# adaLN vectors in small turns between the projections, and w_o's first weights loaded before the attention

## The chip, the cores and the metric

The kernel runs on one NeuronCore of a Trainium2 chip. The metric is the device time of one execution in microseconds. Three runs of the kernel before took 2390.59, 2391.88 and 2393.76 us, median 2391.88.

## The reference, cut to what matters

Two layers over 1024 latent tokens of width 1024. Each layer modulates its input with vectors made from the condition, mixes tokens, adds and normalises, and does the same once more with a SwiGLU feed-forward. Layer 0 mixes by differential attention over 256 context tokens and the 1024 latent ones, layer 1 by pooling.

```
def adaln_params(cond, w_mod, b_mod):
    m = silu(cond) @ w_mod + b_mod                 # 1024 -> 6 * 1024
    return split(m, 6)                             # shift, scale, gate, twice
for i in (0, 1):
    sh1, sc1, g1, sh2, sc2, g2 = adaln_params(c, w_mod[i], b_mod[i])
    hx = x * (1 + sc1) + sh1
    if i == 0:
        csh1, csc1, ... = adaln_params(c_ctx, w_mod[0], b_mod[0])
        hc = ctx * (1 + csc1) + csh1
        k, v = project of hc (256 tokens) and hx (1024 tokens);  q = project of hx
        q, k (latent part) = rope(q), rope(k)
        per head: o = softmax(q1 k1) v - lam * softmax(q2 k2) v   # 8 heads, 2 maps of 64 features
        y = (rms_norm(o) * subln_g * 0.2) @ w_o
    else:
        y = pooling(hx)
    x = layer_norm(ALPHA * x + g1 * y)
    x = layer_norm(ALPHA * x + g2 * swiglu(x * (1 + sc2) + sh2))
```

## The kernel before, in words

Features lie on the partitions and tokens along the free axis. Every fp32 operand of a large product is split into a high part (a cast to fp32r) and a low part (the rest), and a product is three matmuls, high by high, high by low and low by high. A weight tile of 1024 x 128 gives 8 x 3 = 24 matmuls for a span of 512 tokens; this is called a product here.

The stages follow one another: a start in which the latent tokens are modulated and the first keys and queries are made beside it; the projections, a list `steps` of (kind, group, spans) with kind 0 for q, 1 for k and 2 for v; the attention over 8 heads; w_o; the feed-forward, then layer 1. Before the change `steps` takes the rest of q group 0, then groups 1 and 2 of q, half of v, the context and latent spans of k, q group 3 and the other half of v. The weights of a step come through `split_w` (L130): a load of 512 KB from SP into `wr` (two buffers), the high part `wh` on ACT, the low part `wl` on DVE. `finish_qk` (L178) does the rotary on DVE (`ta`, `tb`) and GpSimd, splits the result into `ot` and stores it from ACT's queue. Products go into 8 PSUM banks with the tag `mm`, which `pg` below shares.

Twelve of layer 0's adaLN vectors' pieces of 512 columns, the first four for c_ctx and eight for c, are made between the projections. `between()` (L284) is called after each span and at two of the ten token tiles of v. It takes one piece from the list `rest` and calls `gemv_half` (L102): four loads of 512 KB of `gw`, two buffers; eight operations on DVE (L112 the first, L114 the others) that add w_mod's rows times the condition into `gacc`; four matmuls `pg` (L117) with a matrix of ones that add gacc over the partitions; and an addition on DVE (L118). With the fifth call `context()` modulates the context tokens.

In the attention pools `pq` and `pb` hold kk, qd, vv and the work tiles. When it ends these are released, and pools `pz` (with zT, 4 MB), `phx` and `pf` take memory. `raw` (4 buffers of 512 KB, for w_o's and the feed-forward's weights and for layer 1's gw) and `aop` (3 buffers, the split weights made by `form`) are in `pf`, so `w_o` (L609) first loads and forms weights when the attention's memory is free. w_o goes by d, 128 output features at a time; layer 1's pieces `gemv1(0)` and `gemv1(1)` stand behind d = 1 and d = 4.

The source is not the order of the program. A scheduler puts each engine's instructions in an order of its own, in which each engine works strictly one after the other, and pools decide which tile lies on which memory; an instruction waits for whoever last used its buffer. Loads are issued by SP, the projections' stores by ACT.

Of the kernel before, what the change touches and what calls it, by code (L numbers as in the profile page):

```python
# [43 lines left out]
def backbone(ctx: ExitStack, tc: tile.TileContext, a: dict, out: bass.AP):  # L44
# [56 lines left out]

    def gemv_half(pool, psum, pstag, l, b, tags, bufs, j=0):  # L102

        acc = pool.tile([P, 512], F32, name="gacc", tag=tags[0], bufs=bufs[0])
        for k2 in range(KT // 2):
            wt = pool.tile([P, 2, 512], F32, name="gw", tag=tags[1], bufs=bufs[1])
            SP.dma_start(wt, a["w_mod"][l, k2 * 2 * P:(k2 + 1) * 2 * P, b * 512:(b + 1) * 512]
                         .rearrange("(k p) f -> p k f", p=P))
            for i in range(2):
                k = 2 * k2 + i  # L110
                if k == 0:
                    V.tensor_scalar(acc, wt[:, i, :], sc_sb[:, 0, j:j + 1], None, ALU.mult)  # L112
                else:
                    V.scalar_tensor_tensor(acc, wt[:, i, :], sc_sb[:, k, j:j + 1], acc, ALU.mult, ALU.add)  # L114
        pg = psum.tile([P, 4, P], F32, name="pg", tag=pstag)
        for i in range(4):
            PE.matmul(pg[:, i, :], lhsT=acc[:, i * P:(i + 1) * P], rhs=ones_f, start=True, stop=True)  # L117
        V.tensor_tensor((modx if j else modv[l])[:, b * 4:(b + 1) * 4], pg[:, :, 0], bmod[:, l, b * 4:(b + 1) * 4], ALU.add)  # L118

# [3 lines left out]
    with ExitStack() as actx:  # L123
# [28 lines left out]
        def project_v(g, parts):  # L152
            for tt in list(range(2, NTT)) + [0, 1]:
                if tt in (4, 7):
                    between()
                ts_ = slice(tt * P, (tt + 1) * P)
                ps = psA.tile([P, 512], F32, name="mm", tag="mm")
                for k in range(KT):
                    wh, wl = parts[k]
                    PE.matmul(ps, lhsT=hT_hi[:, k, ts_], rhs=wh, start=(k == 0), stop=False)  # L160
                    PE.matmul(ps, lhsT=hT_hi[:, k, ts_], rhs=wl, start=False, stop=False)  # L161
                    PE.matmul(ps, lhsT=hT_lo[:, k, ts_], rhs=wh, start=False, stop=(k == KT - 1))  # L162
                vt = pa.tile([P, 4, P], F32, name="vt", tag="vt", bufs=3)
                S.copy(vt, ps.rearrange("p (h e) -> p h e", e=P))
                S.dma_start(v_d[g][:, :, tt].rearrange("h p e -> p h e"), vt)
# [37 lines left out]
        def project_qk(kind, g, spans, w):  # L203
            for (t0, n) in spans:
                pp = []
                for s in range(2):
                    ps = psA.tile([P, 512], F32, name="mm", tag="mm")
                    for k in range(KT):
                        mm3(ps, w[s], k, t0, n)
                    pp.append(ps)  # L210
                finish_qk(kind, g, t0, n, pp)
                between()

# [67 lines left out]

        rest = [(b, 1) for b in range(4)] + [None] + [(b, 0) for b in range(4, 12)]

        def between():  # L284
            if rest:
                v = rest.pop(0)
                if len(rest) == 10:
                    load_context()
                if v is None:
                    context()  # L290
                else:
                    gemv_half(pa, psA, "mm", 0, v[0], ("gacc", "gw"), (2, 2), v[1])
# [32 lines left out]
    with ExitStack() as bctx:  # L325
# [90 lines left out]
        for h in range(NH):  # L416
# [54 lines left out]
    def parts(hi, lo, src, eng=None):
        S.copy(hi, src)  # L472
        (eng or V).tensor_tensor(lo, src, hi.bitcast(F32), ALU.subtract)  # L473

    def form(src):

        t = pf.tile([P, 2, 4, P], F32R, name="aop", tag="aop", bufs=AOP)
        parts(t[:, 0], t[:, 1], src)
        return t

# [349 lines left out]
    def pool_group(t0, n, g):  # L830
# [156 lines left out]
```

## Time and profile before

| | |
|---|---|
| median of 3 runs | 2391.88 us |
| profiled execution | 2393.9 us, of which the span from first to last instruction is 2392.1 |
| TensorE matmul busy | 2262.7 us, 95% of the span |
| VectorE busy | 1704.9 us, 71% |
| ScalarE, GpSimd busy | 932.9 us, 39%; 624.5 us, 26% |
| mean DMA rate over the span | 99 GB/s |
| chain of waits, by engine | PE 77%, DVE 13%, DMA 5% |

L12 is line 12 of the kernel. PE is TensorE, DVE is VectorE, ACT is ScalarE, POOL is GpSimd and SP is SyncE, which issues loads. The chain is the work that ended last, followed back from the end; its shares say how much of the span each engine or line had on that path. A timeline row gives the start, the time of a run of like instructions, and in brackets how long the engine was idle before it and whose end released it. PEclk is the granted clock of TensorE as a share of 2.4 GHz.

### The profile page before, as it was taken

What the parts mean: (1) busy time and instruction counts of PE and PEld (TensorE: products, weight loads), DVE (VectorE), ACT (ScalarE), POOL (GpSimd) and SP (SyncE); (2) the same over time, 40 slices, a digit from 0 to 9 for tenths busy, and PEclk for the clock granted to TensorE, in tenths of its full rate; (3) what the DMA queues carried; (4) which work ended last, traced back from release to release, by engine and by line L of the source; (5) the groups of instructions that cost most, each with busy time, mean ns of one, the idle gap of its engine ahead of it and who ended that gap; (6) DMA issues with size and microseconds to landing.
All of it is one profiled execution on the core that took longest, in us unless ns stands there. A gap on an engine that the chain in (4) does not pass through costs nothing.

```text
span 2392.1 us, 31056 instructions
## 1 busy us (share of the span) xinstructions
PE 2262.7 (95%) x11800; PEld 1924.2 (80%) x11800; DVE 1704.9 (71%) x2580; ACT 932.9 (39%) x1635; POOL 624.5 (26%) x618
## 2 busy tenths in 40 slices
PE   5879899999999997999999999999799999999997
PEld 4668787999999786888888888898588888888886
DVE  7664622899998589777777777767966666666678
ACT  3213112787877265222222222437522222222242
POOL 3432322444444043111111111202511111111122
PEclk9989999999999999999999999999899999999999
DMA  7767636523321431322222222213011111111121
GB/s 265 239 210 221 208 87 180 171 69 109 89 78 36 150 114 58 112 88 88 86 84 86 83 85 88 88 33 90 21 62 53 53 51 51 51 52 54 53 89 71
DMA packets 100918, 236.64 MB, mean 99 GB/s; under 512 B 9376, under 2 KB 27424, under 8 KB 99616
## 3 DMA queue, kind: packets, MB, share of 16 engines
q1 hardware_dynamic: 78688, 210.53, 27.7%
q10 hardware_dynamic: 22080, 24.12, 3.5%
q8 instruction: 93, 1.52, 0.3%
q14 instruction: 57, 0.47, 0.1%
HBM read 206.30 MB, written 28.31 MB: 98 GB/s over the span
## 4 chain that ended last, share of the span: by engine, by line
PE 77%; DVE 13%; DMA 5%; ACT 2%; issue 2%; POOL 1%; DVEq 0%; ACTq 0%; SPq 0%; POOLq 0%
PE mm L598 18%; PE mm L597 18%; PE mm L596 18%; PE s L345 6%; PE misc L376 6%; DMA gw<-in_w_mod 3%; PE misc L369 3%; DVE gacc L114 2%; PE mm L161 1%; PE mm L162 1%; PE mm L160 1%; DVE zT L601 1%; DVE aop L473 1%; DVE acc L236 1%; PE mm L170 1%
## 5 line engine op out<-in xcount | busy, mean ns | idle before, releaser
L596 PE MATMUL mm<-H,aop 128*128 128x512 f32 x1232 | 483.6, 393 | 18.0 <-ACT aop L472 10.5
L598 PE MATMUL mm<-H,aop 128*128 128x512 f32 x1232 | 481.8, 392 | 7.1 <-DVE aop L473 7.1
L597 PE MATMUL mm<-H,aop 128*128 128x512 f32 x1232 | 482.6, 392 | 3.3 <-DVE H L473 3.3
L472 ACT CAST aop<-raw 128x512 fp32r<-128x512 f32 x392 | 241.9, 621 | 618.3 <-PE mm L598 577.5
L601 DVE SCALAR_TENSOR_TENSOR zT<-mm,g,zT 128x512 f32<-128x512 f32 (+1 forms) x400 | 276.6, 703 | 123.3 <-PE mm L598 121.2
L473 DVE TENSOR_TENSOR aop<-raw,aop 128x512 fp32r<-128x512 f32 x392 | 278.2, 712 | 86.9 <-ACT aop L472 85.8
L596 PEld LDWEIGHTS mm<-H,aop 128*128 128x128 f32 x1232 | 232.9, 189 | 68.6 <-ACT aop L472 13.2
L598 PEld LDWEIGHTS mm<-H,aop 128*128 128x128 f32 x1232 | 232.6, 189 | 57.8 <-DVE aop L473 9.8
L597 PEld LDWEIGHTS mm<-H,aop 128*128 128x128 f32 x1232 | 232.9, 189 | 52.3 <-DVE H L473 4.5
L348 DVE TENSOR_REDUCE mx<-s 128x1 f32<-128x1280 f32 x128 | 190.6, 1490 | 68.5 <-PE s L345 63.6
L597 PE MATMUL mm<-quad,aop 128*128 128x512 f32 x608 | 237.7, 391 | 1.4 <-DVE quad L473 1.4
L596 PE MATMUL mm<-quad,aop 128*128 128x512 f32 x608 | 237.6, 391 | 0.4 <-ACT aop L472 0.4
L598 PE MATMUL mm<-quad,aop 128*128 128x512 f32 x608 | 236.3, 389 | 0.0
L114 DVE SCALAR_TENSOR_TENSOR gacc<-gw,sc_sb,gacc 128x512 f32<-128x512 f32 x168 | 154.7, 921 | 57.9 <-DMA gw<-in_w_mod 54.7
L345 PE MATMUL s<-kk,qd 128*128 128x512 f32 (+1 forms) x768 | 180.0, 369 | 4.3 <-ACT e L351 4.3
L351 ACT ACTIVATE e<-s,mx 128x1280 f32<-128x1280 f32 x128 | 170.1, 1329 | 20.8 <-DVE mx L348 20.7
L674 POOL TENSOR_TENSOR raw<-s,raw 128x512 f32<-128x512 f32 x40 | 52.0, 1300 | 450.4 <-DVE aop L473 321.5
L345 PEld LDWEIGHTS s<-kk,qd 128*128 128x128 f32 x768 | 134.8, 189 | 27.8 <-ACT e L351 5.3
L376 PE MATMUL misc<-vv,at 128*128 128x128 f32 x1280 | 153.5, 275 | 0.6 <-ACT at L370 0.6
L376 PEld LDWEIGHTS misc<-vv,at 128*128 128x128 f32 x1280 | 148.0, 192 | 0.8 <-ACT at L370 0.8
L354 POOL TENSOR_SCALAR e<-e,sm 128x1280 f32<-128x1280 f32 x64 | 88.2, 1379 | 229.5 <-DVE sm L352 225.6
L597 PEld LDWEIGHTS mm<-quad,aop 128*128 128x128 f32 x608 | 114.1, 188 | 28.4 <-DVE quad L473 5.2
(171 smaller groups left out, 4087.6 us busy)
## 6 DMA issues: line engine op xcount, KB each, us to landing
gw<-in_w_mod SPq DMA_DIRECT2D x96, 512.0 KB, 4.3
raw<-in_w_in SPq DMA_DIRECT2D x88, 512.0 KB, 3.6
raw<-in_w_out SPq DMA_DIRECT2D x48, 512.0 KB, 3.5
qd<-q_d SPq DMA_DIRECT2D x64, 256.0 KB, 5.6
raw<-in_w_o SPq DMA_DIRECT2D x24, 512.0 KB, 3.6
kk<-k_d SPq DMA_DIRECT2D x8, 1280.0 KB, 6.8
wr<-in_w_qk SPq DMA_DIRECT2D x18, 512.0 KB, 5.5
wm<-in_w_mod SPq DMA_DIRECT2D x8, 1024.0 KB, 7.3
```

What stands on the lines that cost most here:

```text
L114: V.scalar_tensor_tensor(acc, wt[:, i, :], sc_sb[:, k, j:j + 1], acc, ALU.mult, ALU.add)
L345: PE.matmul(ps[:, lo_:hi_], lhsT=self.qd[:, m, s, q0:q0 + P], rhs=self.kk[:, m, lo_:hi_], start=(s == 0), stop=(s == 1))
L348: V.tensor_reduce(mx, ps[:, 0:TA], axis=AX.X, op=ALU.max, negate=True)
L351: S.activation(e, ps[:, 0:TA], AF.Exp, bias=mx, accum_out=sm)
L354: G.tensor_scalar(e, e, sm, 1.0, ALU.mult, ALU.mult)
L376: PE.matmul(av, lhsT=self.at[:, kb, :], rhs=self.vv[:, kb, :], start=(kb == 0), stop=(kb == NTT - 1))
L472: S.copy(hi, src)
L473: (eng or V).tensor_tensor(lo, src, hi.bitcast(F32), ALU.subtract)
L596: PE.matmul(p_, lhsT=wh, rhs=xh, start=first, stop=False)
L597: PE.matmul(p_, lhsT=wh, rhs=xl, start=False, stop=False)
L598: PE.matmul(p_, lhsT=wl, rhs=xh, start=False, stop=last)
L601: V.scalar_tensor_tensor(zT[:, d, cs], p_, gate[:, d:d + 1], zT[:, d, cs], ALU.mult, ALU.add)
```

## The change

`between()` is replaced by 48 `turn()`s. One turn is called after each product of q and k (inside `project_qk`) and before each token tile of v, and does a quarter of a piece: it issues one load of gw and adds two operations to gacc. gw has four buffers, and three loads are issued ahead. The matmuls pg and the addition of a finished piece (`sum_rows`, L293) come at the turn after. The pieces for c_ctx come first, the loads of the context tokens at turn 12 and `context()` at turn 16. `steps` now takes all of q first, then half of v, the keys, and the other half of v.

A new pool `pwt` holds raw and aop, 28 KB of each partition, and is opened ahead of the attention's pools. w_o's first four raw loads (`raw_o`) and the first forms stand in the source at the end of the attention's loop; `w_o` takes them from the lists `wo_raw` and `wo_form`. `gemv_half` now serves layer 1 only.

```
     def gemv_half(pool, psum, pstag, l, b, tags, bufs, wpool):
...
         def project_v(g, parts):
             for tt in list(range(2, NTT)) + [0, 1]:
-                if tt in (4, 7):
-                    between()
+                turn()
...
         def project_qk(kind, g, spans, w):
...
                     pp.append(ps)
+                    turn()
                 finish_qk(kind, g, t0, n, pp)
-                between()
...
-        rest = [(b, 1) for b in range(4)] + [None] + [(b, 0) for b in range(4, 12)]
-
-        def between():
-            if rest:
-                v = rest.pop(0)
-                if len(rest) == 10:
+        GWL = 3
+        turns = [(b, k2, 1) for b in range(4) for k2 in range(4)] + [(b, k2, 0) for b in range(4, 12) for k2 in range(4)]
+        loaded, todo = [], []
+
+        def load_rows():
+            if len(loaded) < len(turns):
+                b, k2, _ = turns[len(loaded)]
+                loaded.append(pa.tile([P, 2, 512], F32, name="gw", tag="gw", bufs=GWL + 1))
+                SP.dma_start(loaded[-1], a["w_mod"][0, k2 * 2 * P:(k2 + 1) * 2 * P, b * 512:(b + 1) * 512]
+                             .rearrange("(k p) f -> p k f", p=P))
+
+        def sum_rows():
+
+            acc, b, j = todo.pop()
+            pg = psA.tile([P, 4, P], F32, name="pg", tag="mm")
+            for i in range(4):
+                PE.matmul(pg[:, i, :], lhsT=acc[:, i * P:(i + 1) * P], rhs=ones_f, start=True, stop=True)
+            V.tensor_tensor((modx if j else modv[0])[:, b * 4:(b + 1) * 4], pg[:, :, 0], bmod[:, 0, b * 4:(b + 1) * 4], ALU.add)
...
+        def turn():
+            if todo:
+                sum_rows()
+                if done[0] == 12:
                     load_context()
-                if v is None:
+                if done[0] == 16:
                     context()
+            if done[0] == len(turns):
+                return
+            b, k2, j = turns[done[0]]
+            load_rows()
+            wt = loaded[done[0]]
+            for i in range(2):
+                k = 2 * k2 + i
+                if k == 0:
+                    accs[0] = pa.tile([P, 512], F32, name="gacc", tag="gacc", bufs=2)
+                    V.tensor_scalar(accs[0], wt[:, i, :], sc_sb[:, 0, j:j + 1], None, ALU.mult)
                 else:
-                    gemv_half(pa, psA, "mm", 0, v[0], ("gacc", "gw"), (2, 2), v[1])
+                    V.scalar_tensor_tensor(accs[0], wt[:, i, :], sc_sb[:, k, j:j + 1], accs[0], ALU.mult, ALU.add)
+            if k2 == 3:
+                todo.append((accs[0], b, j))
+            done[0] += 1
+
+        steps = [(0, 0, SPANS[1:2])] + [(0, g, SPANS[0:2]) for g in range(1, 4)] + [(2, 0, None), (1, 0, SPANS[2:])]
+        steps += [(1, g, SPANS) for g in range(1, 4)] + [(2, 1, None)]
+        for _ in range(GWL):
+            load_rows()
...
+    pwt = ctx.enter_context(tc.tile_pool(name="pwt", bufs=1, reuse_waits="tile"))
+
+    def raw(shape):
+        return pwt.tile(shape, F32, name="raw", tag="raw", bufs=RAW)
...
+        wo_raw = [raw_o(d) for d in range(RAW)]
+        wo_form = [form(wo_raw[0][:, 4 * q:4 * q + 4]) for q in range(2)]
...
     def w_o(d, t0, n):
-        wr = raw([P, KT, P])
-        SP.dma_start(wr, a["w_o"][d])
+        wr = wo_raw.pop(0) if wo_raw else raw_o(d)
...
-            w = form(wr[:, 4 * q:4 * q + 4])
+            w = wo_form.pop(0) if wo_form else form(wr[:, 4 * q:4 * q + 4])
```

VectorE's order in the q part, before, from the end of the piece that c_ctx's second sum closes. L114 and L112 add into gacc, L118 is the addition behind pg, L191 and L192 are the rotary and L54 splits a weight's low half wl.

```order
L112 TENSOR_SCALAR gacc<-gw,sc_sb 128x512
L114 SCALAR_TENSOR_TENSOR gacc<-gw,sc_sb,gacc 128x512
L118 TENSOR_TENSOR modx<-pg,bmod 128x4
L114 SCALAR_TENSOR_TENSOR gacc<-gw,sc_sb,gacc 128x512 x4
L191 TENSOR_TENSOR ta<-mm,cosT 128x512 x2
L192 TENSOR_TENSOR tb<-mm,sinT 128x512 x2
L114 SCALAR_TENSOR_TENSOR gacc<-gw,sc_sb,gacc 128x512
L54 TENSOR_TENSOR wl<-wr,wh 128x1024
L114 SCALAR_TENSOR_TENSOR gacc<-gw,sc_sb,gacc 128x512
L112 TENSOR_SCALAR gacc<-gw,sc_sb 128x512
L114 SCALAR_TENSOR_TENSOR gacc<-gw,sc_sb,gacc 128x512
L118 TENSOR_TENSOR modx<-pg,bmod 128x4
```

The same place after the change, from the addition L299 behind the second sum's pg on; L320 and L322 add into gacc, L190 and L191 are the rotary, L141 splits a q weight.

```order
L299 TENSOR_TENSOR modx<-pg,bmod 128x4
L320 TENSOR_SCALAR gacc<-gw,sc_sb 128x512
L322 SCALAR_TENSOR_TENSOR gacc<-gw,sc_sb,gacc 128x512 x7
L190 TENSOR_TENSOR ta<-mm,cosT 128x512 x2
L191 TENSOR_TENSOR tb<-mm,sinT 128x512
L141 SCALAR_TENSOR_TENSOR wl<-wr,wh 128x1024
L191 TENSOR_TENSOR tb<-mm,sinT 128x512
L190 TENSOR_TENSOR ta<-mm,cosT 128x512 x2
```

Eight gacc operations now stand in one block behind the addition L299, and the low half of a weight behind that block; before, two to six operations stood between such additions and a split.

VectorE's order at the first weights of v after the change, from v's first low half (L54) to its second; L274 is context's addition.

```order
L54 TENSOR_TENSOR wl<-wr,wh 128x1024
L191 TENSOR_TENSOR tb<-mm,sinT 128x512
L320 TENSOR_SCALAR gacc<-gw,sc_sb 128x512
L322 SCALAR_TENSOR_TENSOR gacc<-gw,sc_sb,gacc 128x512 x7
L299 TENSOR_TENSOR modx<-pg,bmod 128x4
L320 TENSOR_SCALAR gacc<-gw,sc_sb 128x512
L274 TENSOR_SCALAR modx<-modx 128x8
L322 SCALAR_TENSOR_TENSOR gacc<-gw,sc_sb,gacc 128x512 x6
L190 TENSOR_TENSOR ta<-mm,cosT 128x512 x2
L54 TENSOR_TENSOR wl<-wr,wh 128x1024
```

Fifteen gacc operations and an addition L299 that waits for pg stand between the two low halves of the first v weights.

SP's order around the attention's start, before: L132 are v's last weights, L107 loads gw, and kk, qd and vv are the first heads' keys, queries and values.

```order
L132 DMA wr<-in_w_v 128x1024
L107 DMA gw<-in_w_mod 128x2x512 x4
L132 DMA wr<-in_w_v 128x1024 x3
L419 DMA kk<-k_d_86 128x2x1280
L425 DMA qd<-q_d_82 64x2x512 x4
L431 DMA vv<-v_d_90 128x1280
L425 DMA qd<-q_d_82 64x2x512 x4
```

After the change, from the last gw loads of the projections (L290) on; L373 loads w_o's weights and L107 is layer 1's first gw.

```order
L132 DMA wr<-in_w_v 128x1024
L290 DMA gw<-in_w_mod 128x2x512 x4
L132 DMA wr<-in_w_v 128x1024
L290 DMA gw<-in_w_mod 128x2x512 x4
L373 DMA raw<-in_w_o 128x1024 x4
L107 DMA gw<-in_w_mod 128x2x512
L474 DMA kk<-k_d_86 128x2x1280
L480 DMA qd<-q_d_82 64x2x512 x4
L486 DMA vv<-v_d_90 128x1280
```

Four raw loads of w_o and a first load of layer 1's gw now stand ahead of kk. The eight loads of zT stood further down, behind the second head's first loads (L605); they left that place.

SP's order around the attention's end, before, from the last head's queries on.

```order
L431 DMA vv<-v_d_91 128x1280
L425 DMA qd<-q_d_85 64x2x512 x4
L611 DMA raw<-in_w_o 128x1024 x2
L107 DMA gw<-in_w_mod 128x2x512 x4
L611 DMA raw<-in_w_o 128x1024 x3
L107 DMA gw<-in_w_mod 128x2x512 x4
L611 DMA raw<-in_w_o 128x1024 x19
```

After the change.

```order
L480 DMA qd<-q_d_85 64x2x512 x4
L486 DMA vv<-v_d_91 128x1280
L480 DMA qd<-q_d_85 64x2x512 x4
L650 DMA zT<-in_xT 128x1024 x8
L107 DMA gw<-in_w_mod 128x2x512 x3
L373 DMA raw<-in_w_o 128x1024
L107 DMA gw<-in_w_mod 128x2x512 x4
L373 DMA raw<-in_w_o 128x1024 x19
```

The eight loads of zT (L650, 4 MB) now stand behind the last head's queries, ahead of w_o's fifth weight and of layer 1's gw.

## Rows read from the trace of the kernel before

**Rows 1.** Page, chain that ended last, shares of the span by line.

```profile
PE mm L598 18%; PE mm L597 18%; PE mm L596 18%; PE s L345 6%; PE misc L376 6%; DMA gw<-in_w_mod 3%; PE misc L369 3%; DVE gacc L114 2%; PE mm L161 1%; PE mm L162 1%; PE mm L160 1%; DVE zT L601 1%; DVE aop L473 1%; DVE acc L236 1%; PE mm L170 1%
```

**Rows 2.** Stretches: busy us (instructions) per engine, PEclk, DMA share, GB/s.

```profile
75.00:100.00 25.00, 20.10 (x83) 16.51 (x82) 18.34 (x25) 5.08 (x8) 12.28 (x10) 0.86 0.80 253
...
75.00:200.00 125.00, 104.11 (x431) 85.18 (x430) 83.00 (x105) 16.05 (x26) 45.15 (x32) 0.89 0.70 219
...
200.00:250.00 50.00, 50.00 (x260) 42.95 (x259) 22.58 (x29) 19.74 (x33) 9.11 (x9) 1.00 0.73 229
...
250.00:300.00 50.00, 40.57 (x218) 35.27 (x217) 32.03 (x44) 7.93 (x14) 18.88 (x13) 0.93 0.69 203
```

**Rows 3.** Waits, 60 to 300 us: us in total, times, longest us.

```profile
DVE gacc L114 <- DMA gw<-in_w_mod: 45.8, 20, 5.0
...
PE pg L117 <- DVE gacc L114: 26.7, 7, 5.5
...
PE mm L161 <- DVE wl L54: 3.6, 1, 3.6
```

**Rows 4.** TensorE timeline: start, us, instruction, [idle before <-releaser].

```profile
105.81 1.69 PE L117 MATMUL pg<-ones_f,gacc 128*128 128x128 f32 x8 [3.88 <-DVE gacc L114]
...
107.72 0.63 PE L171 MATMUL mm<-hT_lo,wh 128*128 128x512 f32 x1
...
108.15 0.63 PE L172 MATMUL mm<-hT_hi,wl 128*128 128x512 f32 x1
...
113.64 0.39 PE L172 MATMUL mm<-hT_hi,wl 128*128 128x512 f32 x1
...
119.08 0.39 PE L172 MATMUL mm<-hT_hi,wl 128*128 128x512 f32 x1
...
164.32 1.05 PE L117 MATMUL pg<-ones_f,gacc 128*128 128x128 f32 x8
```

**Rows 5.** VectorE by line and form, 95 to 300 us: busy us, mean ns.

```profile
L114 DVE SCALAR_TENSOR_TENSOR gacc<-gw,sc_sb,gacc 128x512 f32<-128x512 f32 x76 | 71.8, 945 | 47.4 <-DMA gw<-in_w_mod 45.8
...
L54 DVE TENSOR_TENSOR wl<-wr,wh 128x1024 fp32r<-128x1024 f32 x12 | 17.4, 1455 | 18.3 <-ACT wh L136 18.3
...
L191 DVE TENSOR_TENSOR ta<-mm,cosT 128x512 f32<-128x512 f32 x20 | 13.1, 681 | 0.0
...
L112 DVE TENSOR_SCALAR gacc<-gw,sc_sb 128x512 f32<-128x512 f32 x10 | 6.5, 651 | 4.9 <-DMA gw<-in_w_mod 4.9
...
L141 DVE SCALAR_TENSOR_TENSOR wl<-wr,wh 128x1024 fp32r<-128x1024 f32 x2 | 3.5, 1752 | 0.0
```

**Rows 6.** VectorE, then GpSimd timeline near 98 us.

```profile
98.21 4.35 DVE L114 SCALAR_TENSOR_TENSOR gacc<-gw,sc_sb,gacc 128x512 f32<-128x512 f32 x3
...
104.21 1.54 DVE L114 SCALAR_TENSOR_TENSOR gacc<-gw,sc_sb,gacc 128x512 f32<-128x512 f32 x2 [1.66 <-DMA gw<-in_w_mod]
...
98.23 2.99 POOL L195 TENSOR_TENSOR ot<-ta,ot 128x512 fp32r<-128x512 f32 x2
```

**Rows 7.** SyncE timeline, first head's queries.

```profile
378.67 15.75 SPq L425 DMA_DIRECT2D qd<-q_d  x4
```

**Rows 8.** TensorE timeline, end of the projections.

```profile
402.27 2.46 PE L345 MATMUL s<-kk,qd 128*128 128x512 f32 x12
```

**Rows 9.** Page, DMA issues: count, KB each, median us to landing.

```profile
gw<-in_w_mod SPq DMA_DIRECT2D x96, 512.0 KB, 4.3
...
qd<-q_d SPq DMA_DIRECT2D x64, 256.0 KB, 5.6
...
kk<-k_d SPq DMA_DIRECT2D x8, 1280.0 KB, 6.8
```

**Rows 10.** TensorE timeline, first w_o matmul.

```profile
787.13 0.80 PE L596 MATMUL mm<-onH,aop 128*128 128x512 f32 x1 [1.28 <-ACT aop L472]
```

**Rows 11.** DMA, 420 to 460 us, GB/s in 40 slices of 1 us.

```profile
GB/s 215 157 81 176 163 270 250 199 195 328 397 397 418 418 430 414 422 401 279 127 20 0 0 0 0 0 159 379 430 394 268 250 238 227 29 10 0 0 0 0
```

**Rows 12.** Stretch of w_o's start, columns as in rows 2.

```profile
790.00:820.00 30.00, 30.00 (x137) 25.01 (x136) 20.38 (x32) 6.22 (x10) 0.00 (x0) 0.96 0.75 243
```

More of the change, by code (lines that the diff above doesn't have):

```diff
@@ L100, in backbone, with gemv_half @@
     v_d = [dram.tile([4, P, NTT, P], F32, name=f"v_d{g}", tag=f"v_d{g}") for g in range(2)]
-    def gemv_half(pool, psum, pstag, l, b, tags, bufs, j=0):
+    def gemv_half(pool, psum, pstag, l, b, tags, bufs, wpool):
         acc = pool.tile([P, 512], F32, name="gacc", tag=tags[0], bufs=bufs[0])
         for k2 in range(KT // 2):
-            wt = pool.tile([P, 2, 512], F32, name="gw", tag=tags[1], bufs=bufs[1])
+            wt = wpool.tile([P, 2, 512], F32, name="gw", tag=tags[1], bufs=bufs[1])
             SP.dma_start(wt, a["w_mod"][l, k2 * 2 * P:(k2 + 1) * 2 * P, b * 512:(b + 1) * 512]
@@ L111, in gemv_half @@
                 if k == 0:
-                    V.tensor_scalar(acc, wt[:, i, :], sc_sb[:, 0, j:j + 1], None, ALU.mult)
+                    V.tensor_scalar(acc, wt[:, i, :], sc_sb[:, 0, 0:1], None, ALU.mult)
                 else:
-                    V.scalar_tensor_tensor(acc, wt[:, i, :], sc_sb[:, k, j:j + 1], acc, ALU.mult, ALU.add)
+                    V.scalar_tensor_tensor(acc, wt[:, i, :], sc_sb[:, k, 0:1], acc, ALU.mult, ALU.add)
         pg = psum.tile([P, 4, P], F32, name="pg", tag=pstag)
@@ L117, in gemv_half @@
             PE.matmul(pg[:, i, :], lhsT=acc[:, i * P:(i + 1) * P], rhs=ones_f, start=True, stop=True)
-        V.tensor_tensor((modx if j else modv[l])[:, b * 4:(b + 1) * 4], pg[:, :, 0], bmod[:, l, b * 4:(b + 1) * 4], ALU.add)
+        V.tensor_tensor(modv[l][:, b * 4:(b + 1) * 4], pg[:, :, 0], bmod[:, l, b * 4:(b + 1) * 4], ALU.add)
     with ExitStack() as actx:
@@ new lines, in sum_rows @@
+        def sum_rows():
[4 more added lines that the diff above has]
+            V.tensor_tensor((modx if j else modv[0])[:, b * 4:(b + 1) * 4], pg[:, :, 0], bmod[:, 0, b * 4:(b + 1) * 4], ALU.add)
+        done = [0]
+        accs = [None]
+        def turn():
+            if todo:
+                sum_rows()
+                if done[0] == 12:
@@ L288, in between @@
                     load_context()
-                if v is None:
+                if done[0] == 16:
                     context()
-                else:
-                    gemv_half(pa, psA, "mm", 0, v[0], ("gacc", "gw"), (2, 2), v[1])
-        steps = [(0, 0, SPANS[1:2]), (0, 1, SPANS[0:2]), (0, 2, SPANS[0:2]), (2, 0, None), (1, 0, SPANS[2:]), (1, 1, SPANS),
-                 (1, 2, SPANS), (1, 3, SPANS), (0, 3, SPANS[0:2]), (2, 1, None)]
+            if done[0] == len(turns):
+                return
@@ L319, in backbone, with parts, form, raw_o @@
     phh = ctx.enter_context(tc.tile_pool(name="phh", bufs=1, side="right", reuse_waits="tile"))
+    pwt = ctx.enter_context(tc.tile_pool(name="pwt", bufs=1, reuse_waits="tile"))
+    def raw(shape):
+        return pwt.tile(shape, F32, name="raw", tag="raw", bufs=RAW)
+    def parts(hi, lo, src, eng=None):
+        S.copy(hi, src)
+        (eng or V).tensor_tensor(lo, src, hi.bitcast(F32), ALU.subtract)
+    def form(src):
+        t = pwt.tile([P, 2, 4, P], F32R, name="aop", tag="aop", bufs=AOP)
+        parts(t[:, 0], t[:, 1], src)
+        return t
+    def raw_o(d):
+        wr = raw([P, KT, P])
+        SP.dma_start(wr, a["w_o"][d])
+        return wr
     sg = ctile([P, 1], "sg")
@@ L454, in backbone @@
     chunk = [slice(0, 512), slice(512, 1024)]
-    def raw(shape):
-        return pf.tile(shape, F32, name="raw", tag="raw", bufs=RAW)
     def ct():
@@ L469, in row_tile @@
         return pf.tile([P, D], F32, name="xn", tag="quad", bufs=QD)
[L471 to L479, printed above, removed]
     def ln_rows(t, dst):
@@ L622, in gemv1 @@
     def gemv1(b):
-        gemv_half(pf, psL, "ln", 1, b, ("gacc", "raw"), (1, RAW))
+        gemv_half(pf, psL, "ln", 1, b, ("gacc", "raw"), (1, RAW), wpool=pwt)
     for d in range(KT):
@@ L837, in pool_group @@
         else:
-            pt = [pf.tile([P, 2, 512], F32R, name="pt", tag="aop", bufs=AOP) for _ in range(2)]
+            pt = [pwt.tile([P, 2, 512], F32R, name="pt", tag="aop", bufs=AOP) for _ in range(2)]
         if t0 == 768:
```

## The prediction

> **What bounds the kernel now.** I read the page's chain of waits first, for which waits lie on the path [rows 1]: matmul lines lead it, and of what is not a matmul the loads of gw (slices of the adaLN weight matrix) and the sum made from them, gacc, come early. The table of stretches says where [rows 2]: from 75 to 300 us TensorE misses 20.9 us (125 − 104.1) and 9.4 us (50 − 40.6), between them, from 200 to 250, nothing. The list of waits of that stretch names the cause [rows 3]: 7 times pg, the matmuls that add gacc over the partitions, waited for gacc, 26.7 us together, and once a projection waited 3.6 us for its weights' low half: 30.3 us. gacc itself waits for loads (20 times, 45.8 us), since gw has two buffers.
>
> TensorE pays again after each stop. In its timeline [rows 4] pg comes after 3.88 us of nothing and takes 1.69 us, against 1.05 at 164.32 where it comes unstalled; the next matmuls start 0.43 us apart (107.72, 108.15), later 0.2265 (24 of them from 113.64 to 119.08). The granted clock of such stretches is 0.86 to 0.93 against 1.00 [rows 2], which is time spent at 1.2 instead of 2.4 GHz. Six to nine matmuls at the long pitch cost 6 to 9 × 0.20 us, most often with 0.6 on pg: near 1.6 us a stop, 7 stops, 11 us. The stops cost **30.3 + 11 = 41.3 us** in all.
>
> **What is removed.** A sum's pg now stands behind one more product of 24 matmuls, 24 × 0.2265 = 5.4 us, and gw has four buffers with three loads ahead. Neither the 48 loads nor the 96 operations on gacc nor the pg matmuls go away, they move. Where each stop was at most 5.5 us [rows 3] and DVE gets its data earlier, I let all eight stops go. What is late next is the question.
>
> **What is added between the projections.** In DVE's order the small turns do not stay small: eight gacc operations stand in one block behind L299, the addition that waits for pg, and the weights' low halves stand behind that block. DVE can't begin the block before TensorE reached pg, and TensorE soon needs the weight. Two places follow.
> - Behind the second sum: TensorE has 26 matmuls from pg to the first that reads wl, the low half of a q weight, 26 × 0.2265 = 5.9 us. DVE has one L112 (0.65), seven L114 (0.945 each, 6.6), three rotary products (0.68 each, 2.0) and the split (1.75), by the means of [rows 5]: 11.0 us. Stall 11.0 − 5.9 = 5.1 us. By the shortest row, two L114 in 1.54 [rows 6], DVE takes 9.8 us and the stall is 3.9. By the longest, three in 4.35, it is 1.45 × 7 + 4.4 = 14.6 us, stall 8.7. I take 5.1, from the means of this very stretch.
> - Behind the fourth sum: from pg to the first matmul that reads a low half of v's weights are 15 matmuls, 3.4 us. Behind L299 stand one L112, six L114, two rotary products and the split L54: 0.65 + 5.7 + 1.4 + 1.45 = 9.2 us (a 128x8 operation among them left out). Stall 5.8, from 4.8 to 8.9 by the same two rows.
> - Elsewhere in the q part I count 1 us (0 to 2.5), and for the low clock after the two stops 2 × 1.7 = 3.4. In the k part and the last v I find DVE a product or more ahead: 0.
> Together 5.1 + 5.8 + 1 + 3.4 = **15.3 us**.
>
> The spread of L114 is itself a row: three take 4.35 us from 98.21 while GpSimd works from 98.23, two take 1.54 from 104.21 with GpSimd idle [rows 6]. The Trainium skill, "SBUF — State Buffer", section Who interferes with whom, says that a DVE instruction with both inputs in SBUF and a GpSimd instruction that reads SBUF shut each other out, and that the one that issues first holds. The trace agrees; by the rule a block of eight that starts beside the rotary halves on GpSimd costs 14.6 instead of 11.0 us, and the sum would be 3.6 us worse.
>
> **The first head.** Before, the first qd pieces were issued from 378.67 us [rows 7], kk just ahead of them, 24 us before the first score at 402.27 ends the projections [rows 8]. Now kk stands in SP's queue behind four raw loads and a gw load that waits until two forms of w_o exist, and ACT makes these after the eighth of ten vt copies; I get an issue about 7 us before the end. The first qd pieces wait for a buffer that overlaps the last v weights, and come free 18 matmuls, 4.1 us, before the end. With 6.8 and 5.6 us to landing [rows 9] kk lands at the end, qd at +1.5, four pieces at about +2. **+2 us**, between 0 and +5.5. Below 0 is excluded, since before TensorE came to the score without a gap.
>
> **w_o.** The first form is ready when the attention ends, so the 1.28 us wait before the first w_o matmul goes [rows 10]; the stop on GpSimd before it stays, and with it the low clock. But the 28 KB taken ahead move the attention's pools up, and zT now lies under them: its eight loads, 4 MB, leave the attention's start for its end, ahead of gw x3, raw (d = 4), gw x4 and raw (d = 5) on SP. That is 17 pieces of 512 KB before d = 5 can be formed. zT's rate when it ran alone was 397 to 430 GB/s [rows 11], 1.25 us a piece; gw and raw among matmuls I set at 1.9, and at most at the 2.16 us that 243 GB/s give [rows 12]. 8 × 1.25 + 9 × 1.9 + 4 (first landing, [rows 9]) = 31.1 us, against a need at 5 × 5.44 + 2.4 + 1.6 = 31.2 us (five products, the low clock, two pg). So it just fits: 0, and the other end, all at 2.16, is +9.7. With −1.3 and a share for the tightness, **0 us**, between −2.5 and +8.
>
> The Trainium skill, "DMA: Bandwidth & Descriptors", section Where 436 GB/s comes from, sets about 358 GB/s as the limit from HBM for one core; the row shows up to 430, so here the measurement decides. By the page's figure, as an estimate, zT's eight pieces would take 1.7 us longer and the sum would grow by as much.
>
> **Sum.** −41.3 + 15.3 + 2 + 0 = −24.0 us. The profiled execution took 2393.9 us (span 2392.1 and 1.8 around it), 2.0 above the median of the runs shown; so 2370 in such an execution and 2391.9 − 24.0 = **2368 us** as a median. With new stalls from 10 to 24, the first head 0 to 4 and w_o −1 to +4: 2360 to 2382.
>
> **Rivals.**
> - *No new stop.* DVE finishes each block in time because loads ahead let it start early. For it: from 200 to 250 us TensorE is full while 229 GB/s move [rows 2]. Against: L299 waits for pg by the order itself. Then −41.3 − 1.3 + 1: 2350 us.
> - *Transfers bind.* From 75 to 200 us 219 × 125 = 27.4 MB moved. 20 us less for the same bytes is 261 GB/s, a little over the highest stretch of 25 us, 253, at a DMA share of 0.80 [rows 2]. For it: never seen higher there. Against: the share leaves room, and zT ran at 430. If 219 is the ceiling, only 250–300 us gains, 9.4 + 3.5, less 2 for the first head: 2381 us.
> - *Loads at the attention's end decide*: slower. zT's 4 MB push w_o's fifth weight out. With p us a piece the stall is 17p + 4 − 31; from p = 3.0 (175 GB/s) it eats the 24.0. For it: loads held by buffers ran at 203 GB/s over 250 to 300 [rows 2], 2.6 us a piece, and one at a time takes 4.3 us to land [rows 9]. Against: 243 at this very place [rows 12]. At 3.5 us, between those two, the stall is 32.5: 2400 us.
> - *The change does not do what it says*: since the sums are emitted in blocks of eight, pg still waits for gacc as often and as long. For it: the order's blocks. Against: the product now between. Then the stops stay, and 2391 us.
>
> **How the numbers follow.** Forecast 0.60; no new stop 0.16; transfers 0.10; attention's end 0.09; no effect 0.05. About 0.2%, 4.8 us, is what a measurement here can tell from no change, so "same" is 2387.1 to 2396.7. Faster: 0.60 + 0.16 + 0.09 of the transfers' case = 0.85; same 0.05 + 0.01 = 0.06; slower 0.09. Left out of 2352 to 2388: the attention's end 0.09, no effect 0.05 and the lowest third of no new stop, 0.06.
>
> **What would show it.** In the timeline of TensorE up to the attention: no idle before pg; two stops of 4 to 9 us, both for a weight's low half from DVE, one in a q product behind the second sum, one in v's first product; the end of the projections near 376 us. At the attention's start a wait for qd or kk of about 2 us. At its end the eight zT loads in SP's queue and no stop of over 4 us in w_o. I am wrong if pg still waits for gacc, if the stretches from 75 to 180 us show a DMA share of 0.9, or if w_o waits for raw.

## The result, and the profile after

The changed kernel took 2367.44 us (median of 4 runs, 2365.28 to 2370.8), against 2391.24 for the kernel before (2390.44 to 2393.76): a ratio of 0.990, 95% interval 0.9883 to 0.9917. The forecast was 2368. The profiled execution took 2367.97 us, its span is 2366.2, 25.9 shorter than before.

TensorE's timeline of the changed kernel, with the columns of [rows 4]. Up to 378 us are the projections and the first scores, the last two rows are w_o.

```profile
132.03 0.80 PE L171 MATMUL mm<-hT_hi,wl 128*128 128x512 f32 x1 [3.28 <-DVE wl L141]
...
162.76 0.50 PE L159 MATMUL mm<-wh,hT_hi 128*128 128x512 f32 x1 [1.72 <-DVE modx L299]
...
173.07 0.80 PE L160 MATMUL mm<-wl,hT_hi 128*128 128x512 f32 x1 [7.98 <-DVE wl L54]
...
372.75 0.39 PE L161 MATMUL mm<-wh,hT_lo 128*128 128x512 f32 x1
...
375.14 1.39 PE L400 MATMUL s<-kk,qd 128*128 128x512 f32 x6 [2.00 <-DMA qd<-q_d]
...
377.32 3.03 PE L400 MATMUL s<-kk,qd 128*128 128x512 f32 x7 [0.80 <-DMA qd<-q_d]
...
760.07 0.77 PE L641 MATMUL mm<-onH,aop 128*128 128x512 f32 x1
...
790.50 1.13 PE L117 MATMUL pg<-ones_f,gacc 128*128 128x128 f32 x8 [0.48 <-DVE gacc L114]
```

No pg has an idle time in the projections; the three stops left are 3.28, 1.72 and 7.98 us, two of them for a weight's low half; at the third a product of v waits for a PSUM bank that the addition L299 frees. The last projection matmul starts at 372.75, so the projections end at 372.98 instead of 402.27 [rows 8]. Then the first score waits 2.00 and 0.80 us for qd. The first w_o matmul, at 760.07, has no idle time before it, where 1.28 us lay [rows 10].

Two of the waits up to 385 us after, with the columns of [rows 3].

```profile
DVE modv L299 <- PE pg L298: 53.9, 6, 20.7
...
DVE modx L299 <- PE pg L298: 23.5, 3, 11.5
```

The two have changed places. Before, pg waited 26.7 us for gacc on VectorE; now VectorE waits 53.9 and 23.5 us for pg on TensorE, which costs nothing by itself, but all that stands behind L299 waits with it.

The stretches, columns as in [rows 2].

```profile
75.00:100.00 25.00, 25.00 (x117) 20.84 (x115) 17.79 (x27) 5.03 (x7) 13.24 (x10) 1.00 0.83 267
...
75.00:200.00 125.00, 112.03 (x495) 92.06 (x494) 72.47 (x99) 24.59 (x35) 53.32 (x38) 0.96 0.72 227
...
250.00:300.00 50.00, 50.00 (x275) 43.64 (x274) 32.04 (x43) 8.71 (x14) 15.89 (x12) 1.00 0.80 249
```

From 75 to 200 us TensorE is busy 112.0 us instead of 104.1, at a clock of 0.96 instead of 0.89, and the transfers go up by 8 GB/s only. From 250 to 300 us it misses nothing.

| stretch | before | after | difference |
|---|---|---|---|
| start to the end of the projections | 402.27 | 372.98 | −29.3 |
| to the first w_o matmul | 384.86 | 387.09 | +2.2 |
| to the end of the span | 1604.97 | 1606.13 | +1.2 |

The last stretch lies between 1603.0 and 1608.5 us in the profiles of the experiments, whatever was edited ahead of it; so its 1.2 us can't be told from no difference.

### The profile page after: what moved, and what is told of

Its sections match the earlier page's. It is cut to its first block, busy times and chain, and to the rows that moved or that the text cites. A ratio compares the mean times of both kernels' runs of the same rounds, so it can differ in the third digit from the quotient of the medians.

```text
span 2366.2 us, 31051 instructions
## 1 busy us (share of the span) xinstructions
PE 2251.8 (95%) x11800; PEld 1916.2 (81%) x11800; DVE 1695.7 (72%) x2580; ACT 932.7 (39%) x1635; POOL 617.3 (26%) x618
## 4 chain that ended last, share of the span: by engine, by line
PE 84%; DVE 11%; DMA 1%; ACT 1%; issue 1%; POOL 1%; SPq 0%; DVEq 0%; ACTq 0%; POOLq 0%
PE mm L643 18%; PE mm L642 18%; PE mm L641 18%; PE s L400 6%; PE misc L431 6%; PE misc L424 3%; PE mm L171 2%; PE mm L170 2%; PE mm L169 2%; PE mm L160 1%; PE mm L161 1%; PE mm L159 1%; DVE aop L363 1%; DVE zT L646 1%; DVE acc L235 1%
## 5 line engine op out<-in xcount | busy, mean ns | idle before, releaser
L642 PEld LDWEIGHTS mm<-quad,aop 128*128 128x128 f32 x608 | 114.2, 188 | 28.5 <-DVE quad L363 5.3
L641 PEld LDWEIGHTS mm<-quad,aop 128*128 128x128 f32 x608 | 114.2, 188 | 24.4 <-ACT aop L362 0.9
```

The source lines that it names most:

```text
L641: PE.matmul(p_, lhsT=wh, rhs=xh, start=first, stop=False)
L642: PE.matmul(p_, lhsT=wh, rhs=xl, start=False, stop=False)
```

## The experiments

The question is less whether the forecast held than which of the change's parts did it: the two halves of the change, pg's later place, the buffers of gw, or the pace of the pieces; and what the three stops that are left hang on. Each ratio is to the kernel before.

**The turns alone.** raw, form and pt stay in pf:

```
-    pwt = ctx.enter_context(tc.tile_pool(name="pwt", bufs=1, reuse_waits="tile"))
...
-        wo_raw = [raw_o(d) for d in range(RAW)]
-        wo_form = [form(wo_raw[0][:, 4 * q:4 * q + 4]) for q in range(2)]
```

> The turns between the projections as in the changed kernel, but raw, form and the pool pt stay in pf and w_o loads and forms its first weights after the attention, as before. Theory (the two parts add up, the turns carry all of the gain, the early w_o loads nothing): the projections still end near 373 us with stops of 3 to 4 and 7 to 9 us for weights' low halves; no wait for qd before the first score (it was 2.00 and 0.80 us with the change), the eight zT loads back at the attention's start, w_o's first matmul again about 1.7 us after the last transposition. 2367.4 - 2.8 + 1.3 - 1.2 = 2365, between 2362 and 2368. Rival (w_o's early weights give part of the 24 us): 2370 to 2378.

2366.21 us (2364.86 to 2367.83), ratio 0.9888 (0.9872 to 0.9903): as the theory had it. The projections end at 372.2 us, the first score waits 0.68 us instead of 2.8, the first w_o matmul waits 1.28 us again.

**The early w_o weights alone.** The pool and the early loads as changed, `between()` and `gemv_half` as before.

> Only the other part: the pool pwt ahead of the attention, w_o's four loads and first forms early, layer 1's gw in it; between the projections all as before. Theory: pg waits for gacc as before (near 27 us), a wait for qd at the first score of about 3 us, zT's loads behind the attention, 0 to 1 us of stop in w_o: 2391.2 + 2.8 - 1.3 + 1.2 = 2394, between 2391 and 2397. Rival (the early loads are a gain of their own): 2389 or less.

2395.76 us (2393.24 to 2398.07), ratio 1.0012 (1.0003 to 1.0022). The first score waits 1.24 us behind an early form on ScalarE and 0.76 for qd. So this half costs about 3 us alone, in line with the theory; with the run before, all of the gain is the turns'.

**pg put off, nothing else.** The kernel before, where each `between()` first does the pg of the piece summed ahead of it:

```
+            if late:
+                gemv_sum(psA, "mm", 0, *late.pop())
             if rest:
```

> The kernel before with one edit: each between() first does the pg matmuls and the addition of the piece that the between() ahead of it summed, so a sum has a whole span (48 matmuls, 10.9 us) more. gw keeps two buffers, the steps and the pools are as before. Theory (the place of pg is what stopped TensorE): the waits of pg for gacc go from 26.7 us to under 3, new waits for weights of at most 12 us, projections end at 370 to 382 us, 2360 to 2372 us in all. Rival (loads with two buffers are the limit, so that the wait only moves): pg or the weights still wait 15 us or more, 2378 or more.

2400.48 us (2398.28 to 2404.2), ratio 1.0031 (1.0022 to 1.0041): the theory fell, the rival held in its time. Three of TensorE's twelve stops, and VectorE around the first two of them:

```profile
115.89 0.50 PE L176 MATMUL mm<-hT_hi,wh 128*128 128x512 f32 x1 [3.86 <-DVE ta L197]
...
135.78 0.80 PE L176 MATMUL mm<-hT_hi,wh 128*128 128x512 f32 x1 [6.18 <-DVE ta L197]
...
299.23 2.08 PE L123 MATMUL pg<-ones_f,gacc 128*128 128x128 f32 x8 [6.97 <-DVE gacc L114]
```

```profile
111.13 1.54 DVE L114 SCALAR_TENSOR_TENSOR gacc<-gw,sc_sb,gacc 128x512 f32<-128x512 f32 x2 [3.43 <-DMA gw<-in_w_mod]
...
127.93 3.11 DVE L114 SCALAR_TENSOR_TENSOR gacc<-gw,sc_sb,gacc 128x512 f32<-128x512 f32 x4 [4.40 <-DMA gw<-in_w_mod]
...
133.77 0.75 DVE L114 SCALAR_TENSOR_TENSOR gacc<-gw,sc_sb,gacc 128x512 f32<-128x512 f32 x1 [2.73 <-DMA gw<-in_w_mod]
...
134.44 1.28 DVE L197 TENSOR_TENSOR ta<-mm,cosT 128x512 f32<-128x512 f32 x2
```

In all TensorE idles 35.0 us up to the first score, against 30.3. In five of the stops pg still waits for gacc, 14.8 us together. Where pg no longer waits, the next product does: it wants a PSUM bank that the rotary (ta) has to free, and ta stands in VectorE's queue behind gacc operations that wait for gw. A later pg by itself moves part of the wait and saves nothing.

**Two buffers for gw**, all else as changed (`GWL = 1` in place of 3).

> The changed kernel with gw back at two buffers (one load ahead in place of three); turns, steps and pools as changed, pg at the same distance of 96 projection matmuls. The run that put off pg alone kept its stops, so what counts is either the spread of a piece over four products (21.8 us in place of 10.9) or the loads ahead. Theory (spread): pg waits under 3 us in all, two or three stops for weights, 2364 to 2374 us. Rival (loads ahead): waits of TensorE rise by 10 us or more, 2376 or more.

2370.65 us (2369.52 to 2372.69), ratio 0.9906 (0.9892 to 0.9921): the loads ahead are worth some 3 us or nothing, not the 24. The theory's time held, its stops did not. The wait of the sums for their loads, up to 378 us, columns as in [rows 3]:

```profile
DVE gacc L322 <- DMA gw<-in_w_mod: 40.2, 15, 5.5
```

With four buffers this wait is 2.8 us. TensorE's stops in the projections come to 12.3 us all the same, against 13.0, at other places: no low half stops it for more than 0.64 us, but a pg waits 4.82 us for a bank that the rotary frees, and a product 4.67 us for the context's modulation on ScalarE. So at this pace sums that wait for their loads need not stop TensorE.

**A piece in two products, with four buffers.** Each turn does two quarters. In the q part that is the pace of the kernel before; in v, where that made two pieces in ten products, it is faster than before:

```
         def turn():
+            quarter()
+            quarter()
+
+        def quarter():
             if todo:
```

> The changed kernel with each turn doing two quarters of a piece, so that a piece is made every two products (10.9 us) as before the change, with four gw buffers and three loads ahead. Theory (spread): the loads of gw want 2.1 MB in each 10.9 us again, 193 GB/s beside weights and stores, and TensorE stops 15 us or more up to 200 us: 2376 or more. Rival (loads ahead): stops as in the changed kernel, 2362 to 2372.

2396.96 us (2395.07 to 2400.81), ratio 1.0013 (1.0003 to 1.0022): all of the gain is gone. The projections end at 397.96 us, 25.0 later than with the change, and the first score waits 6.94 us for qd, 4.1 more. TensorE stops seven times in the projections, 30.9 us in all. Three of these stops, and the stretch from 75 to 200 us:

```profile
138.11 0.80 PE L171 MATMUL mm<-hT_hi,wl 128*128 128x512 f32 x1 [6.03 <-DVE wl L141]
...
178.06 0.80 PE L298 MATMUL pg<-ones_f,gacc 128*128 128x128 f32 x2 [7.35 <-DVE gacc L326]
...
187.49 0.79 PE L160 MATMUL mm<-wl,hT_hi 128*128 128x512 f32 x1 [8.63 <-DVE wl L54]
```

```profile
75.00:200.00 125.00, 97.94 (x430) 80.28 (x429) 100.36 (x130) 24.95 (x42) 57.36 (x42) 0.88 0.78 255
```

255 GB/s moved at a share of 0.78, more than in the same stretch of either kernel, and TensorE was busy 97.9 us, less than in either. So the gain hangs on the pace: one piece, 2.1 MB of w_mod, in four products (21.8 us, 96 GB/s) in place of two (10.9 us, 193 GB/s). In TensorE's order the last piece's pg stood 912 matmuls into the 1440 of the projections before, stands 744 in here and 1296 in with the change.

The pace could act through the transfers or through VectorE's queue. Here are the sums from 75 to 200 us with the columns of [rows 5], before, with the change, and in this run:

```profile
L114 DVE SCALAR_TENSOR_TENSOR gacc<-gw,sc_sb,gacc 128x512 f32<-128x512 f32 x52 | 49.4, 950 | 29.4 <-DMA gw<-in_w_mod 28.4
...
L322 DVE SCALAR_TENSOR_TENSOR gacc<-gw,sc_sb,gacc 128x512 f32<-128x512 f32 x41 | 35.8, 877 | 3.8 <-DMA gw<-in_w_mod 2.8
...
L326 DVE SCALAR_TENSOR_TENSOR gacc<-gw,sc_sb,gacc 128x512 f32<-128x512 f32 x68 | 65.8, 972 | 4.0 <-DMA gw<-in_w_mod 2.1
```

The sums waited 28.4 us for gw before and 2.1 us here, and TensorE stops as long, 22.5 of the 30.9 us behind a weight's low half that VectorE makes. By the means of this run, as an estimate, VectorE has 11.7 us of work in the q part for every 10.9 us of TensorE: eight operations on gacc (7.6), four rotary products (2.7) and a split (1.4); with the change, four operations on gacc make it 7.6. That speaks for VectorE's queue; it is argued, since no run narrowed the sums at this pace. Nor did a run keep the slow pace with pg at its old place or with the old order of `steps`, so whether the pace alone is enough is not shown.

**v's low halves on GpSimd**, to take the split out of VectorE's queue:

```
-                sub_hi(wl, wr, wh)
+                (eng or V).tensor_tensor(wl, wr, wh.bitcast(F32), ALU.subtract)
...
-                wh, wl = split_w([P, 2, 512], a["w_v"][g, :, 2 * k2:2 * k2 + 2, :])
+                wh, wl = split_w([P, 2, 512], a["w_v"][g, :, 2 * k2:2 * k2 + 2, :], eng=G)
```

> The changed kernel, with the low half of v's weights made by GpSimd in place of VectorE, so that it does not stand behind the gacc block. Theory (the 7.98 us stop at 173 us is the queue on VectorE): that stop falls to 0 to 4 us, the low clock behind it with it, 2358 to 2364 us. Rival (the weight or the gacc loads come late, so that v's first product waits anyway): the stop stays within 2 us of 8 and the time at 2366 to 2370.

2371.95 us (2366.95 to 2375.27), ratio 0.991 (0.9888 to 0.9931). The stop stayed, at 6.92 us, now released by GpSimd:

```profile
171.21 1.27 POOL L192 TENSOR_TENSOR ta<-ta,tb 128x512 f32<-128x512 f32 x1 [11.03 <-DVE ta L190]
...
172.44 2.34 POOL L137 TENSOR_TENSOR wl<-wr,wh 128x1024 fp32r<-128x1024 f32 x1
```

GpSimd waited 11.03 us for ta on VectorE, and the split stood behind that. So the split was still behind the gacc block, by a detour, and this run could not tell the theory from the rival.

**Narrow sums.** Seven of eight operations on gacc work on 64 of 512 columns, so that the sums are not the reference's; loads and waits stay:

```
-                    V.scalar_tensor_tensor(accs[0], wt[:, i, :], sc_sb[:, k, j:j + 1], accs[0], ALU.mult, ALU.add)
+                    V.scalar_tensor_tensor(accs[0][:, 0:64], wt[:, i, 0:64], sc_sb[:, k, j:j + 1], accs[0][:, 0:64], ALU.mult, ALU.add)
```

> The changed kernel with seven of eight operations on gacc working on 64 of the 512 columns (the sums are then not those of the reference), all loads, orders and waits as they are. Theory (the weights' low halves stop TensorE because VectorE is busy with the gacc block): the stops of 3.3, 1.7 and 8.0 us go to 0, 0 and at most 2, the low clock behind them too: 2350 to 2357. Rival (the split of v's second weight waits for ScalarE's cast, which is queued behind four stores): the third stop stays at 5 us or more, 2357 to 2363.

2363.85 us (2361.85 to 2366.36), ratio 0.9877 (0.9862 to 0.9893). The first stop fell from 3.28 to 0.52 us and the second went: those came from VectorE's work. The third stayed:

```profile
165.83 0.80 PE L160 MATMUL mm<-wl,hT_hi 128*128 128x512 f32 x1 [7.45 <-DVE wl L54]
```

```profile
159.42 0.61 DVE L322 SCALAR_TENSOR_TENSOR gacc<-gw,sc_sb,gacc 128x64 f32<-128x64 f32 x2 [2.88 <-DMA gw<-in_w_mod]
...
160.80 0.60 DVE L322 SCALAR_TENSOR_TENSOR gacc<-gw,sc_sb,gacc 128x64 f32<-128x64 f32 x2 [0.77 <-DMA gw<-in_w_mod]
...
162.14 0.61 DVE L322 SCALAR_TENSOR_TENSOR gacc<-gw,sc_sb,gacc 128x64 f32<-128x64 f32 x2 [0.74 <-DMA gw<-in_w_mod]
...
163.86 1.92 DVE L54 TENSOR_TENSOR wl<-wr,wh 128x1024 fp32r<-128x1024 f32 x1
```

VectorE had almost nothing to do and still reached the split at 163.86, since its queue waited 2.88, 0.77 and 0.74 us for loads of gw. ScalarE's cast was not the cause either: it had cast that weight at 150.87. For this stop both the theory and the rival named the wrong thing, and the time lies above both ranges; what is left here is that gacc operations ahead of the split wait for their own loads.

**Three buffers, turns alone** (`GWL = 2`), so that fewer operations are at hand.

> The turns alone (w_o's early weights left out) with three gw buffers in place of four, so that VectorE has at most six operations at hand. Theory (the block of eight is what delays the weights): the stop in the q product goes, the one at v's second weight shrinks from 7.5 by 1 to 3 us, 2358 to 2365. Rival (loads ahead are needed): new waits for gw, 2367 or more.

2368.38 us (2365.78 to 2372.01), ratio 0.9897 (0.988 to 0.9914). The q stop went and the one at v's second weight shrank to 6.32 us, as the theory had it, but a pg waits 4.20 us behind a bank's ta instead: no gain. The time is the rival's, though no new stop of TensorE is put down to a load of gw.

**The fifth piece held.** With the turns alone, the fifth piece's first operation takes its scalar by way of the last low half of v's first weights, times zero:

```
+                if g == 0 and k2 == 3:
+                    held.append(wl)
...
+                    s0 = sc_sb[:, 0, j:j + 1]
+                    if done[0] == 4 * HOLD:                      # HOLD = 4
+                        s0 = pa.tile([P, 1], F32, name="s0", tag="s0")
+                        V.scalar_tensor_tensor(s0, held[0][:, 0, 0:1].bitcast(F32), 0.0, sc_sb[:, 0, j:j + 1], ALU.mult, ALU.add)
-                    V.tensor_scalar(accs[0], wt[:, i, :], sc_sb[:, 0, j:j + 1], None, ALU.mult)
+                    V.tensor_scalar(accs[0], wt[:, i, :], s0, None, ALU.mult)
```

> The turns alone, and the first operation of the fifth piece takes its scalar through a 128x1 operation that reads the last low half of v's first weights (times zero, so the sum is the same): the fifth piece and those behind it can't stand ahead of v's splits on VectorE. Theory (v's second low half waits in VectorE's queue behind gacc operations that wait for their own loads, which is why narrower sums and a split on GpSimd left that stop): the 7.5 us stop at v's second weight goes to at most 1.5, the 1.7 us at the bank of the fourth sum may stay; 2355 to 2361. Rival (the second weight's own load or its cast is late, as the channels are shared with gw): the stop stays at 4 us or more, 2363 to 2368.

2354.72 us (2352.65 to 2358.65), ratio 0.9845 (0.9831 to 0.9859). It beats both kernels and lies just under the theory's range. VectorE's order at v's first weights, and the stretch:

```profile
158.32 0.16 DVE L302 TENSOR_TENSOR modx<-pg,bmod 128x4 f32<-128x4 f32 x1 [5.25 <-PE pg L301]
...
159.79 1.95 DVE L54 TENSOR_TENSOR wl<-wr,wh 128x1024 fp32r<-128x1024 f32 x1
...
171.54 0.15 DVE L326 SCALAR_TENSOR_TENSOR s<-wl,sc_sb 128x1 f32<-128x1 f32 x1
```

```profile
75.00:200.00 125.00, 121.62 (x548) 100.56 (x547) 79.75 (x110) 26.34 (x42) 53.42 (x40) 0.99 0.76 239
```

The second split comes at 159.79, 11.3 us earlier than with the change, 1.5 us behind the fourth sum's addition; the held piece begins at 171.54. No stop stands at v's weights, one of 3.28 us is left in the q part, and the projections end at 360.2 us. That settles the third stop: it was VectorE's queue.

**The fourth piece held** in the same way.

> As the run with the fifth piece held, but the fourth piece is held there, and with it all that follow. Theory: no stop of over 1.5 us in the q part or at v's first weights, and the pieces behind still have 30 products to be spread over: 2352 to 2359. Rival (the pieces bunch up behind v's weights and their loads and operations stop the later part of v or the first keys, or the context comes late): one or more stops of 4 us or more after 180 us, 2360 or more.

2365.41 us (2364.46 to 2368.71), ratio 0.9887 (0.9874 to 0.9901): the rival's time held, its place nearly: it had the stop after 180 us. The q stop goes, but the fourth sum's pg stands inside v's first products and waits 7.39 us at 175 us for a gacc that starts too late.

## Why the prediction was right

The time was within 1 us of the forecast, and the first head and w_o went by its steps. That it was so close is partly luck, since errors offset each other. By the profiles the span fell by 25.9 us where the sum had 24.0: the projections ended 3.3 us earlier than the sum's −26.0 has it, and the rest took 3.4 us longer where the sum had 2. Of the signs, the first new stop stayed under the 4 us named, and the projections ended at 373 instead of 376 us. The sum holds sizes that were off, and it did not name the pace.

| term | forecast | measured |
|---|---|---|
| stops that go | −30.3 | −30.3, no pg idle left |
| low clock that goes | −11 | −14.5 |
| stop behind the second sum | +5.1 | +3.28 |
| stop at v's second low half | +5.8 | +7.98 |
| elsewhere in the q part | +1 | 0 |
| stop at the fourth sum's bank | not named | +1.72 |
| low clock behind new stops | +3.4 | +3.1 |
| first head | +2 | +2.80 |
| w_o | 0 | −1.28 and +0.48 |

*Low clock.* Up to the first score 47 matmuls of 512 columns started at the long pitch before, 10.3 us over 0.2265 each; 14 do now, 3.1 us. With the 4.2 us that the seven stalled pg took beyond 1.05 each, 14.5 us go where I had set 11. My own terms did not give that 11: six to nine times 0.20 and 0.6 on pg are 1.8 to 2.4 us a stop, not near 1.6, and 13 to 17 us for seven. The measured terms add up to −44.8 + 16.1 = −28.7 for the projections, against −29.3; 0.6 us is not accounted for.

*Why the stops go.* I let them all go because pg stands a product later and gw has four buffers. That is not the reason: with pg put off alone, the stops come back at the banks and at pg; with four buffers besides, at two products a piece, pg's own wait falls from 26.7 to 7.7 us, but the weights' low halves stop TensorE instead; and with two buffers nearly all of the gain stays. What the gain needs is the pace, a piece in four products instead of two. The step was right in its size and wrong in its reason; had the turns been half as many, the same argument would have forecast a gain where the run shows none.

*The stop behind the second sum* went as worked out, at the short end. VectorE in the changed kernel from the addition to the split, and then at the fourth sum:

```profile
122.88 0.16 DVE L299 TENSOR_TENSOR modx<-pg,bmod 128x4 f32<-128x4 f32 x1 [8.10 <-PE pg L298]
...
122.96 0.48 DVE L320 TENSOR_SCALAR gacc<-gw,sc_sb 128x512 f32<-128x512 f32 x1
...
123.47 5.48 DVE L322 SCALAR_TENSOR_TENSOR gacc<-gw,sc_sb,gacc 128x512 f32<-128x512 f32 x7
...
128.87 1.28 DVE L190 TENSOR_TENSOR ta<-mm,cosT 128x512 f32<-128x512 f32 x2
...
130.67 1.31 DVE L141 SCALAR_TENSOR_TENSOR wl<-wr,wh 128x1024 fp32r<-128x1024 f32 x1
...
155.32 7.31 DVE L322 SCALAR_TENSOR_TENSOR gacc<-gw,sc_sb,gacc 128x512 f32<-128x512 f32 x7
...
162.62 0.48 DVE L320 TENSOR_SCALAR gacc<-gw,sc_sb 128x512 f32<-128x512 f32 x1
...
163.13 2.33 DVE L322 SCALAR_TENSOR_TENSOR gacc<-gw,sc_sb,gacc 128x512 f32<-128x512 f32 x3
...
166.67 1.54 DVE L322 SCALAR_TENSOR_TENSOR gacc<-gw,sc_sb,gacc 128x512 f32<-128x512 f32 x2 [1.21 <-DMA gw<-in_w_mod]
...
169.24 0.75 DVE L322 SCALAR_TENSOR_TENSOR gacc<-gw,sc_sb,gacc 128x512 f32<-128x512 f32 x1 [1.03 <-DMA gw<-in_w_mod]
...
169.90 1.28 DVE L190 TENSOR_TENSOR ta<-mm,cosT 128x512 f32<-128x512 f32 x2
...
171.10 1.92 DVE L54 TENSOR_TENSOR wl<-wr,wh 128x1024 fp32r<-128x1024 f32 x1
```

From 122.88 to the end of the split at 131.98 are 9.1 us, against the 11.0 that I made from means; the seven L322 took 5.48, the short end of my range. At 155.32 seven of them take 7.31, beside GpSimd:

```profile
154.97 3.17 POOL L194 TENSOR_TENSOR ot<-ta,ot 128x512 fp32r<-128x512 f32 x2
```

The Trainium skill, "SBUF — State Buffer", section Who interferes with whom, has a VectorE instruction with two SBUF inputs and a GpSimd instruction that reads SBUF wait for each other; the two rows agree.

*The stop at v's second weight* had the right place and the wrong content: I let VectorE begin at pg and reckoned operations at 0.945 us. The fourth sum's pg ended at 159.66 us, but its addition came at 162.55, since VectorE was still in the seven operations from 155.32 on; a product that needed that addition's bank stopped for 1.72 us. From there to the split (162.55 to 171.10) VectorE works 6.3 us and idles 1.21 and 1.03 us for gw, and with almost no work in the block the stop was still 7.45 us. It is a queue with work and waits for loads in it, and holding the fifth piece back took the stop away.

*The first head.* SyncE's order of the changed kernel there and at the attention's end:

```profile
364.75 0.38 SPq L107 DMA_DIRECT2D gw<-in_w_mod  x1
...
365.18 0.47 SPq L474 DMA_DIRECT2D kk<-k_d  x1
...
369.09 2.62 SPq L480 DMA_DIRECT2D qd<-q_d  x4
...
760.49 3.93 SPq L650 DMA_DIRECT2D zT<-in_xT  x8
...
764.52 7.28 SPq L107 DMA_DIRECT2D gw<-in_w_mod  x3
...
776.87 0.34 SPq L373 DMA_DIRECT2D raw<-in_w_o  x1
```

kk was issued at 365.18, 7.8 us before the end of the projections, and the first qd pieces at 369.09, 3.9 before, against 7 and 4.1 worked out from the order.

*w_o.* zT's eight loads go out from 760.49, ahead of gw and d = 5. Their rate, 755 to 810 us in 40 slices of 1.375 us:

```profile
GB/s 0 0 0 0 74 295 396 352 405 411 417 423 405 404 411 213 71 313 198 256 259 243 276 372 362 301 334 295 238 250 137 262 33 0 149 250 0 0 194 188
```

404 to 423 GB/s in the seven fullest slices while zT runs, much as at its old place; TensorE never stops for raw in w_o, and one pg waits 0.48 us. The slower rival wanted 175 GB/s as the mean of all seventeen pieces, and its stop did not come. (The prediction's other end, all at 2.16 us, works out at +9.5 instead of +9.7.) Of the 2.2 us more between the projections and w_o, 2.80 − 1.28 = 1.5 are these terms; 0.7 us stays open.

Of the rivals, no new stop failed by three stops, transfers by 255 GB/s in the run with a piece in two products, where the change moves 227 and the ceiling was to be 219, no effect by the stops that went.

## What to carry to other kernels

When a side job runs beside a stage, add up what one step of it asks of each engine's queue and of the transfers, and compare that with the time of the step, before you look at buffers or at the order: with twelve pieces spread over the whole stage the kernel gained 24 us; with a piece in two products and four buffers, or with a later sum alone, it gained nothing. In an engine's queue an operation that waits for a load holds all behind it, so keep a weight's split from standing behind a side job's operations; tying the job's start to that split, with one operation of a single column, gave 10 to 12 us more. A wait that is pushed off one instruction shows up at the next that shares its queue: look for the banks and buffers that the same engine frees.

## What the runs showed of the hardware

A stop costs more than its idle time: before, 30.3 us of stops cost 14.5 us more at a granted clock of 0.86 to 0.93 in the stretches that hold them [rows 2], 0.48 us for each us idle; after, 13.0 us cost 3.1. The same seven operations on gacc took 5.48 us with GpSimd still, and 7.31 us where two operations of GpSimd's, 3.17 us together, began just ahead of them.
